# One gated mixer, regrouped: each output tile behind one block of products, and the next weights' sums in one piece at a block's end

## The chip, the cores and the metric

The kernel runs on one core of one Trainium2 chip. The metric is the device time of one execution in microseconds (us). The kernel before took 2506.31 us in the median of three runs (2504.49 to 2506.65). The engines are named as the profile names them: PE multiplies matrices (PEld loads its weights), DVE and POOL do elementwise work, ACT applies functions and copies, and SP issues the transfers from memory.

## The reference, cut to what matters

The program is one inference step of a decoder trunk of two layers, for 1024 prompt tokens and 64 sample tokens, with 1024 channels. After the token mixer, each layer applies a gated channel mixer:

```python
def swiglu(h, w_in, w_out):
    g, u = jnp.split(h @ w_in, 2, axis=-1)
    return (jax.nn.silu(g) * u) @ w_out

# in each layer, with FFN_DIM = 2816
h = h + mix
h = h + swiglu(rms_norm(h, norm_ffn_g[layer]), w_ffn_in[layer], w_ffn_out[layer])
```

The change concerns this mixer in layer 1 alone, and there only the first group of tokens.

## The kernel before, in words

**Groups and tiles.** The tokens are worked on in two groups: group A, 512 tokens, and group B, 576 tokens. Activations lie with channels on the 128 partitions. The 2816 hidden channels are 22 tiles f of 128; two tiles form a pair q, so there are 11 pairs, 0 to 10. `run_ffn` (L460) loops over the pairs. For each pair it computes both hidden tiles, and then adds the pair before it into the result: the tile `hid` of pair q-1 is multiplied by two output weight tiles of 512 channels (o = 0 and 1). Each of these takes four accumulators of 128 channels, six matmuls of 512 columns each, 24 matmuls for one output tile. DVE adds each accumulator to the running sum `hb` (`added`, L297).

**A block of products.** Group A of layer 1 computes g and u of one hidden tile by a seven-product scheme in place of eight (`strassen`, L518): each product is 12 matmuls of 256 columns (L525), 84 for one block. The seven products land in four accumulator tiles X (two), Y (two), Z (two) and W (one), in this order. DVE combines them by seven additions (`add`, L529), ACT copies one of them out of PSUM first (L541), and ACT applies SiLU at the end (L554). The product of the gate and u (L504) is made on POOL later, by a list of postponed pieces that `flush` empties; a further `flush` copies it into `hid` as a high part (ACT, L240) and a low part (DVE, L241). One flush stands behind X in each block, one in the output part.

**Accumulators.** There are three accumulator buffers in PSUM, taken in turn. W takes X's buffer; the fourth accumulator of an output tile takes the buffer of its first.

**Weights.** SP loads each weight tile (512 KB) into one of four `stage` buffers (L166). The kernel works in float32 split into two parts, so each weight is split before use into a high part (a copy on ACT) and a low part (a subtraction on POOL of the high part from the weight), in one of three `hl` buffers. `w_split` does this. For output weights this is one ACT copy (L184) and two POOL subtractions (L186). For a block of products the weights come as four steps r0 to r3, one for X, Y, Z and W, since the scheme multiplies sums of weights: r0 first needs three sums on DVE (L200, L201, L202) of the two staged tiles g and u, then two copies on ACT (L196) and two subtractions on POOL (L197). r1 and r2 need two of each, r3 one more DVE sum (L214, `sum_c`) and one of each. L186, L197 and L504 are all POOL instructions of 128x512. In all POOL does ten of them for one block and one output tile.

**Order.** Every engine works through its instructions in the order in which the program writes them. `w_next` takes the weights of a step and at the same time writes the splitting of the step two further on. So the r0 of a pair's second block is written at Z of its first block, ahead of the DVE additions there. In the output part a flag, `thin`, makes the three sums of the next r0 single pieces, one behind each of the first three accumulators of the output tile o = 0. The list `seq` fixes the order of the weights, and with it the order of the loads: four loads of input weights for a pair, and then two of output weights.

Layer 0 and group B go through the same functions, but the change leaves their order alone.

Of the kernel before, what the change touches and what calls it, by code (L numbers as in the profile page):

```python
# [57 lines left out]
def trunk_kernel(ctx, tc, x_prompt, x_sample, cache_k, cache_v, state_conformer, state_shortconv, state_pool,  # L58
# [59 lines left out]

    def add_ffn(l, plain, both=True):
        for g in range(NF // 2):  # L120
            for f in (2 * g, 2 * g + 1):
                if f < plain:
                    add_in(w_ffn_in[l], f * 128)
                    add_in(w_ffn_in[l], FFN + f * 128)
                else:
                    a = in_load(w_ffn_in[l], f * 128), in_load(w_ffn_in[l], FFN + f * 128)
                    seq.extend(a + (r,) for r in range(4))
            if g and (g < NF // 2 - 1 or not both):
                for o in range(2):
                    add_out(w_ffn_out[l], g - 1, o)  # L130
        for o in range(2):
            if both:
                add_out(w_ffn_out[l], NF // 2 - 2, o)
            add_out(w_ffn_out[l], NF // 2 - 1, o)
# [87 lines left out]
    def w_next(live=0):  # L222
        j = wj[0]
        wj[0] += 1
        w_split(j + 3 - live)
        w_load(need(j + 6 - live))
        return hls.pop(j)
# [67 lines left out]
    def added(g, dst, acc):  # L295
        for a, d in parts(g, acc, dst):
            dve.tensor_tensor(d, a, d, op=OP.add)  # L297
# [162 lines left out]
    def run_ffn(g, accs, ps, hidp, x, last, sig=False, slot=lambda: None, forms=None, plain=NF,  # L460
# [54 lines left out]

        def strassen(f):  # L518
            w2 = n // 2

            def prod(acc, h, i, b):
                for k in range(4):
                    xk = forms[b](k)
                    for s, (wi, xi) in enumerate(((0, 0), (0, 1), (1, 0))):
                        pe.matmul(acc[:, :w2], h[:, wi, i, k], xk[:, xi], start=k == 0 and s == 0,  # L525
                                  stop=k == 3 and s == 2)

            def add(out, acc, x):
                dve.tensor_tensor(out, acc[:, :w2], x, op=OP.add)  # L529

            a, b = slice(0, w2), slice(w2, n)
            X, h = accs(), w_next()
            prod(X[:, 0], h, 0, "t2")
            prod(X[:, 1], h, 1, "t3")
            flush()
            slot()
            Y, h = accs(), w_next()
            prod(Y[:, 0], h, 0, "t1")
            prod(Y[:, 1], h, 1, "b11")
            G_, U, P = tmp(), tmp(), tmp()  # L540
            act.activation(G_[:, a], Y[:, 1, :w2], AF.Copy)  # L541
            Z, h = accs(), w_next()
            prod(Z[:, 0], h, 0, "t4")
            add(U[:, a], X[:, 0], G_[:, a])
            add(U[:, b], X[:, 1], U[:, a])
            add(P[:, b], Y[:, 0], U[:, b])
            add(G_[:, b], Y[:, 0], U[:, a])
            prod(Z[:, 1], h, 1, "b21")
            W, h = accs(), w_next()
            prod(W[:, 0], h, 0, "b22")  # L550
            add(P[:, a], Z[:, 0], U[:, b])
            add(G_[:, a], Z[:, 1], G_[:, a])
            add(G_[:, b], W[:, 0], G_[:, b])
            act.activation(G_[:, :n], G_[:, :n], AF.Silu)  # L554
            gated(f, P, G_)
            slot()

        for q in range(G + 1):
            if q < G:
                for f in (2 * q, 2 * q + 1):  # L560
                    if f >= plain:
                        if f == plain:
                            forms.get("switch", forms.get("ready"))()
                        strassen(f)
                        continue
                    if f == 0 and not done:
                        run_in(g, accs, x, [ev_g, lambda a: ev_u(0, a)], norm_hooks(g, ps, at=(4, 7)), skew=3)
                        slot()
                        continue
                    one(f, 0)  # L570
                    one(f, 1)
            if q == G - 1:
                free()
                if both:
                    return last([hid.pop(q - 1), hid.pop(q)])
            if q == G:
                flush()
                flush()
                last(hid.pop(q - 1))
            elif q:  # L580
                hh = hid.pop(q - 1)
                for o in range(2):
                    thin[0] = True
                    h = w_next()
                    thin[0] = False
                    for i in range(4):
                        a = accs()
                        out_block(g, a, h, i, hh)
                        added(g, hb[:, o * 4 + i, g.cs], a)
                        if parts_:  # L590
                            parts_.pop(0)()
                        if o == 0 and i == 1:
                            flush()
                        slot()
# [45 lines left out]
    def accs():  # L640
        return accbox["p"].tile([128, len(accbox["g"].blocks), 512], F, name="acc")
# [1392 lines left out]
```

## Time and profile before

| | us |
|---|---|
| median of three runs | 2506.31 |
| the profiled execution, time | 2507.39 |
| the profiled execution, span | 2505.6 |
| PE busy in it | 2420.9 |
| pairs 1 to 9 of layer 1's group A (1742.05 to 2043.17 of the span) | 301.12 |

The pairs 1 to 9 are those that the change reorders. A pair begins where PE begins the 36 matmuls of X and of Y's first product and ends at the same place of the next pair. A row of a timeline gives start, duration, engine, line, operation, what it writes and reads, and a count where several alike are merged; in square brackets stand the idle time before it and what ended it. In a group of instructions the columns behind the count are the total busy time, the mean of one in ns, and the idle time ahead of them with its releasers. Since DVE's and POOL's instructions can hold each other up, the duration that a row gives can include a wait inside the instruction.

### The profile page before, as it was taken

To read this page: it belongs to the slowest core of one execution; us is meant where nothing else is said; L and a number is where in the kernel's file an instruction comes from. 1 tells how busy PE (TensorE), PEld (TensorE's weight loads), DVE (VectorE), ACT (ScalarE), POOL (GpSimd) and SP (SyncE) were. 2 spreads that over 40 slices of the span, in tenths; PEclk is the share of its full clock that TensorE was granted. 3 is DMA by queue.
4 is the path that set the end of the run, shared out by engine and by line. 5 is a ranking of instruction groups with operands and counts; after the bars stand their busy time and mean duration, and the time that the engine had idled before them with its cause. 6 is when DMAs were issued, how large, how long until landed. Compare 5 with 4: busy or idle time off the path is not lost.

```text
span 2505.6 us, 41453 instructions
## 1 busy us (share of the span) xinstructions
PE 2420.9 (97%) x15877; PEld 2190.0 (87%) x15877; DVE 1653.7 (66%) x2288; ACT 1106.5 (44%) x1877; POOL 1625.1 (65%) x1264
## 2 busy tenths in 40 slices
PE   8999999999999999999999999998999999999998
PEld 6788877788777679999999999888888888999998
DVE  3696878977777553766566534458777668666655
ACT  5536876754444343343333422234333444443333
POOL 6764334655654576787787523267888886887775
PEclk9999999999999999999999999999999999999999
DMA  7332231234565534223232311242233323233322
GB/s 226 117 108 73 77 111 48 72 103 144 175 180 172 160 93 148 71 74 98 89 100 86 111 49 43 71 139 68 85 101 102 98 90 92 85 98 114 93 85 81
DMA packets 355485, 258.31 MB, mean 103 GB/s; under 512 B 22913, under 2 KB 303617, under 8 KB 355272
## 3 DMA queue, kind: packets, MB, share of 16 engines
q1 hardware_dynamic: 355256, 255.66, 34.5%
q8 instruction: 126, 2.06, 0.3%
q14 instruction: 71, 0.58, 0.1%
q10 hardware_dynamic: 32, 0.01, 0.0%
HBM read 237.41 MB, written 18.69 MB: 102 GB/s over the span
## 4 chain that ended last, share of the span: by engine, by line
PE 73%; DVE 16%; POOL 4%; issue 3%; ACT 3%; DMA 1%; SPq 0%; DVEq 0%; ACTq 0%; POOLq 0%
PE acc L235 44%; PE acc L525 20%; DVE sum L200 1%; POOL hl L197 1%; DVE hb L297 1%; DVE q L1008 1%; POOL hl L186 1%; PE o L1030 1%; DVE hid L241 1%; PE m L1020 1%; PE m L1132 1%; PE z L991 1%; DVE sum L201 1%; PE z L1155 1%; DVE cacc L831 1%
## 5 line engine op out<-in xcount | busy, mean ns | idle before, releaser
L186 POOL TENSOR_TENSOR hl<-stage,hl 128x512 fp32r<-128x512 f32 x464 | 637.8, 1399 | 389.3 <-ACT hl L184 280.9
L235 PE MATMUL acc<-x,hl 128*128 128x512 f32 (+1 forms) x3648 | 773.5, 350 | 11.2 <-DVE tmp L293 3.0
L235 PEld LDWEIGHTS acc<-x,hl 128*128 128x128 f32 x3648 | 587.9, 190 | 75.1 <-issue 5.8
L235 PE MATMUL acc<-hid,hl 128*128 128x288 f32 (+1 forms) x3096 | 548.2, 333 | 10.8 <-DVE tmp L293 4.6
L235 PEld LDWEIGHTS acc<-hid,hl 128*128 128x128 f32 x3096 | 471.0, 189 | 62.9 <-DVE hb L297 7.2
L297 DVE TENSOR_TENSOR hb<-acc,hb 128x512 f32<-128x512 f32 (+1 forms) x360 | 256.3, 718 | 173.1 <-PE acc L235 171.7
L525 PE MATMUL acc<-x,hl 128*128 128x288 f32 (+1 forms) x2676 | 361.9, 290 | 3.0 <-POOL hl L197 2.4
L525 PEld LDWEIGHTS acc<-x,hl 128*128 128x128 f32 x2676 | 348.6, 188 | 5.3 <-POOL hl L197 3.3
L197 POOL TENSOR_TENSOR hl<-sum,hl 128x512 fp32r<-128x512 f32 x180 | 237.7, 1349 | 169.3 <-ACT hl L196 169.3
L184 ACT ACTIVATE hl<-stage 128x1024 fp32r<-128x1024 f32 x232 | 243.8, 1054 | 228.6 <-PE acc L235 145.8
L529 DVE TENSOR_TENSOR tmp<-acc,tmp 128x288 f32<-128x288 f32 (+1 forms) x420 | 173.6, 441 | 230.6 <-ACT tmp L541 136.2
L197 POOL TENSOR_TENSOR hl<-stage,hl 128x512 fp32r<-128x512 f32 x180 | 268.4, 1513 | 14.4 <-ACT hl L196 14.4
L525 PE MATMUL acc<-b,hl 128*128 128x256 f32 (+1 forms) x1548 | 215.7, 290 | 14.1 <-DVE tmp L529 11.2
L525 PEld LDWEIGHTS acc<-b,hl 128*128 128x128 f32 x1548 | 201.3, 188 | 19.8 <-ACT hl L196 12.6
L235 PE MATMUL acc<-x1t,hl 128*128 128x288 f32 x1152 | 216.3, 296 | 1.5 <-POOL hl L186 1.5
L235 PEld LDWEIGHTS acc<-x1t,hl 128*128 128x128 f32 x1152 | 195.9, 188 | 19.5 <-POOL hl L186 1.8
L196 ACT ACTIVATE hl<-sum 128x512 fp32r<-128x512 f32 x180 | 103.0, 623 | 238.1 <-DVE sum L202 217.6
L293 DVE TENSOR_TENSOR tmp<-acc,rr 128x512 f32<-128x512 f32 (+1 forms) x108 | 75.2, 710 | 136.3 <-PE acc L235 122.4
L196 ACT ACTIVATE hl<-stage 128x512 fp32r<-128x512 f32 x180 | 105.5, 618 | 69.4 <-PE acc L235 59.3
L504 POOL TENSOR_TENSOR tmp<-tmp 128x576 f32<-128x576 f32 (+1 forms) x85 | 126.2, 1485 | 9.2 <-ACT tmp L481 8.2
L252 POOL TENSOR_TENSOR ss<-ss,tmp 128x512 f32<-128x512 f32 (+1 forms) x69 | 108.1, 1566 | 25.5 <-ACT tmp L251 15.2
L235 PE MATMUL acc<-x1a,hl 128*128 128x512 f32 x480 | 121.7, 407 | 2.5 <-POOL hl L186 1.3
(298 smaller groups left out, 3166.5 us busy)
## 6 DMA issues: line engine op xcount, KB each, us to landing
stage<-in_w_ffn_in_dram SPq DMA_DIRECT2D x176, 512.0 KB
stage<-in_w_ffn_out_dram SPq DMA_DIRECT2D x88, 512.0 KB
stage<-in_w_in_even_dram SPq DMA_DIRECT2D x40, 512.0 KB
kst<-in_cache_k_dram SPq DMA_DIRECT2D x64, 256.0 KB
vst<-in_cache_v_dram SPq DMA_DIRECT2D x56, 256.0 KB
stage<-in_w_out_even_dram SPq DMA_DIRECT2D x16, 512.0 KB
stage<-in_w_in_odd_dram SPq DMA_DIRECT2D x16, 512.0 KB
stage<-in_w_out_odd_dram SPq DMA_DIRECT2D x16, 512.0 KB
```

Source lines behind the costliest of these rows:

```text
L184: act.activation(hl[:, 0], st, AF.Copy)
L186: pool.tensor_tensor(hl[:, 1, c], st[:, c], f32(hl[:, 0, c]), op=OP.subtract)
L196: act.activation(hl[:, 0, c], x, AF.Copy)
L197: pool.tensor_tensor(hl[:, 1, c], x, f32(hl[:, 0, c]), op=OP.subtract)
L200: todo = [lambda: dve.tensor_tensor(sb, su[:, lo], su[:, hi], op=OP.add), lambda: dve.tensor_tensor(sa[:, hi], sg[:, lo], su[:, lo], op=OP ...
L235: pe.matmul(acc[:, b, :c1 - c0], w, xs[:, xi, c0 - o:c1 - o], start=first and s == 0, stop=last and s == 2)
L252: pool.tensor_tensor(ss[:, g.cs], ss[:, g.cs], t[:, :g.n], op=OP.add)
L293: dve.tensor_tensor(d, a, r, op=OP.mult)
L297: dve.tensor_tensor(d, a, d, op=OP.add)
L504: (dve if both and f == NF - 1 else pool).tensor_tensor(t[:, :n], t[:, :n], u[:, :n], op=OP.mult)
L525: pe.matmul(acc[:, :w2], h[:, wi, i, k], xk[:, xi], start=k == 0 and s == 0, stop=k == 3 and s == 2)
L529: dve.tensor_tensor(out, acc[:, :w2], x, op=OP.add)
```

## The change

In layer 1's group A, for the pairs 1 to 9:

- Each output tile of pair q-1 stands behind one block of products: the first behind the first block of pair q, the second behind the second (`out_tile`), where both stood behind the second block. `seq`, and so the order of loads, follows: two input tiles, one output tile, and so on.
- The three sums for the next block's r0 are held back at W (`thin`) and written together at the end of the block, behind its seven additions and the SiLU, ahead of the output tile. The copies and the subtractions of r0 follow them there.
- The splitting of r1 is written behind the second accumulator of the output tile, and a flush behind the third.
- In the first block of pair 1 one more flush stands ahead of W, so that pair 0 is in `hid` when the output tile behind that block reads it.

```diff
     def add_ffn(l, plain, both=True):
         for g in range(NF // 2):
+            outs = g and (g < NF // 2 - 1 or not both)
             for f in (2 * g, 2 * g + 1):
 ...
                     seq.extend(a + (r,) for r in range(4))
-            if g and (g < NF // 2 - 1 or not both):
+                if outs and l and both:
+                    add_out(w_ffn_out[l], g - 1, f % 2)
+            if outs and not (l and both):
                 for o in range(2):
                     add_out(w_ffn_out[l], g - 1, o)
 ...
-        def strassen(f):
+        def out_tile(hh, o):
+            h = w_next(1)
+            for i in range(4):
+                a = accs()
+                out_block(g, a, h, i, hh)
+                added(g, hb[:, o * 4 + i, g.cs], a)
+                if i == 1:
+                    w_split(wj[0] + 2)
+                if i == 2:
+                    flush()
+                slot()
+
+        def strassen(f, outs=False):
 ...
             prod(Z[:, 1], h, 1, "b21")
+            if outs and f == 2:
+                flush()
+            thin[0] = outs
             W, h = accs(), w_next()
+            thin[0] = False
 ...
             gated(f, P, G_)
+            if outs:
+                while parts_:
+                    parts_.pop(0)()
             slot()
 
         for q in range(G + 1):
+            alt = done and both and 0 < q < G - 1
 ...
-                        strassen(f)
+                        strassen(f, alt)
+                        if alt:
+                            out_tile(hid[q - 1], f % 2)
                         continue
 ...
+            elif alt:
+                hid.pop(q - 1)
             elif q:
                 hh = hid.pop(q - 1)
```

On DVE, one pair of the kernel before, from the sums that stand ahead of the first block's additions (the names are the tiles: `stage` is a loaded weight tile, `sum` a sum of two, `tmp` the products' combinations, `acc` an accumulator, `hb` the running result):

```order
L200 TENSOR_TENSOR sum_19125<-stage 128x512
L201 TENSOR_TENSOR sum_19124<-stage 128x512
L202 TENSOR_TENSOR sum_19124<-sum_19125,stage 128x512
L529 TENSOR_TENSOR tmp<-acc,tmp 128x256 x7
L214 TENSOR_TENSOR sum_c<-stage,sum_19124 128x512
L529 TENSOR_TENSOR tmp<-acc,tmp 128x256 x7
L297 TENSOR_TENSOR hb<-acc,hb 128x512
L200 TENSOR_TENSOR sum_19313<-stage 128x512
L297 TENSOR_TENSOR hb<-acc,hb 128x512
L201 TENSOR_TENSOR sum_19312<-stage 128x512
L241 TENSOR_TENSOR hid<-tmp,hid 128x512
L297 TENSOR_TENSOR hb<-acc,hb 128x512
```

The third sum (L202) and five more additions to `hb` follow. In the changed kernel, one block and its output tile read so on DVE (L544 is what L529 was, L203 to L205 the three sums, L300 the addition to `hb`, L217 `sum_c`, L244 the low part of `hid`):

```order
L544 TENSOR_TENSOR tmp<-acc,tmp 128x256 x7
L203 TENSOR_TENSOR sum_19160<-stage 128x512
L204 TENSOR_TENSOR sum_19159<-stage 128x512
L205 TENSOR_TENSOR sum_19159<-sum_19160,stage 128x512
L300 TENSOR_TENSOR hb<-acc,hb 128x512 x4
L217 TENSOR_TENSOR sum_c<-stage,sum_19159 128x512
L244 TENSOR_TENSOR hid<-tmp,hid 128x512
```

The sums moved from ahead of seven additions (first block) and from between the additions to `hb` (output part) to one place behind the additions, and every block is like the next.

On POOL, one pair of the kernel before (L197 with `sum` and `stage` are the low parts of r0, r1 and r2, with `sum_c` that of r3, L186 those of the two output weight tiles, L504 the gate times u):

```order
L197 TENSOR_TENSOR hl<-sum_20676,hl 128x512 x2
L197 TENSOR_TENSOR hl<-sum_20677,hl 128x512
L197 TENSOR_TENSOR hl<-stage,hl 128x512 x3
L197 TENSOR_TENSOR hl<-sum_c,hl 128x512
L197 TENSOR_TENSOR hl<-sum_20829,hl 128x512 x2
L197 TENSOR_TENSOR hl<-sum_20830,hl 128x512
L197 TENSOR_TENSOR hl<-stage,hl 128x512 x3
L504 TENSOR_TENSOR tmp<-tmp 128x512
L197 TENSOR_TENSOR hl<-sum_c,hl 128x512
L186 TENSOR_TENSOR hl<-stage,hl 128x512 x4
L504 TENSOR_TENSOR tmp<-tmp 128x512
```

And one block with its output tile in the changed kernel (L200, L189 and L507 are what L197, L186 and L504 were):

```order
L189 TENSOR_TENSOR hl<-stage,hl 128x512 x2
L200 TENSOR_TENSOR hl<-sum_20353,hl 128x512 x2
L200 TENSOR_TENSOR hl<-sum_20354,hl 128x512
L200 TENSOR_TENSOR hl<-stage,hl 128x512
L507 TENSOR_TENSOR tmp<-tmp 128x512
L200 TENSOR_TENSOR hl<-stage,hl 128x512 x2
L200 TENSOR_TENSOR hl<-sum_c,hl 128x512
```

POOL has 20 instructions for a pair in both. Four output-weight subtractions in a row became two and two, each pair of them just ahead of the next r0.

## The prediction

> **What bounds the kernel now.** First the page's head, for the whole program:
>
> ```profile
> span 2505.6 us, 41453 instructions
> PE 2420.9 (97%) x15877; PEld 2190.0 (87%) x15877; DVE 1653.7 (66%) x2288; ACT 1106.5 (44%) x1877; POOL 1625.1 (65%) x1264
> ```
>
> PE is busy nearly throughout, so a change of order can only win back PE's gaps, and only where it acts. So the second view is busy time in windows, one for each of the nine pairs that are reordered, from one pair's first matmul to the next's (columns: length; busy time and count of PE, PEld, DVE, ACT, POOL; clock; transfers):
>
> ```profile
> 1742.05:1777.42 35.37, 33.08 (x222) 29.68 (x221) 25.27 (x35) 15.73 (x27) 32.22 (x23) 1.00 0.31 90
> ...
> 1846.63:1879.08 32.45, 31.82 (x217) 28.81 (x216) 22.28 (x32) 12.94 (x22) 27.93 (x21) 1.00 0.33 98
> 1879.08:1912.36 33.28, 32.24 (x218) 28.78 (x216) 23.65 (x32) 12.94 (x22) 26.95 (x21) 1.00 0.33 96
> ...
> sum 301.12, PE 289.58 PEld 260.31 DVE 216.84 ACT 119.25 POOL 253.83; mean PE 32.18 PEld 28.92 DVE 24.09 ACT 13.25 POOL 28.20
> ```
>
> The nine take 301.12 us, 18 blocks with an output tile of 16.73 each. The clock is 1.00. The three pairs up to 1846.63 take 104.58 and the six behind them 196.54, 32.76 each. What would PE need alone?
>
> ```profile
> 1867.58 11.66 PE L235 MATMUL acc<-hid,hl 128*128 128x512 f32 x48
> 1889.90 4.39 PE L525 MATMUL acc<-x,hl 128*128 128x256 f32 x36
> 1894.12 1.57 PE L525 MATMUL acc<-b,hl 128*128 128x256 f32 x12
> ```
>
> 48 matmuls of 512 columns run from 1867.58 to the pair's end at 1879.08, 11.50 or 0.2396 each; 36 of 256 columns run from 1889.90 to 1894.12, 4.22 or 0.1172 each. One block is 84 x 0.1172 = 9.84, one output tile 24 x 0.2396 = 5.75, both 15.59; 18 of them 280.6, with a few small matmuls of the next group's norm some 282. So 19 us stand between the nine pairs and PE alone: the most that the change can win. The waits of PE's matmuls in these windows name DVE first:
>
> ```profile
> PE acc L525 <- DVE tmp L529: 7.8, 10, 1.7
> PE acc L235 <- DVE hb L297: 2.2, 4, 0.8
> PE acc L525 <- POOL hl L197: 0.9, 2, 0.5
> ```
>
> These 10.9 us are the visible part (weight loads that start late and slower matmuls behind them make the rest). They name W, which waits for DVE to release X's accumulator. But a wait at W is only where PE notices; something has to hold the whole loop at 32.5 to 33.3. The groups of POOL's instructions in these windows show it:
>
> ```profile
> L197 POOL TENSOR_TENSOR hl<-stage,hl 128x512 fp32r<-128x512 f32 x54 | 79.8, 1504 | 0.0
> L197 POOL TENSOR_TENSOR hl<-sum,hl 128x512 fp32r<-128x512 f32 x56 | 77.0, 1405 | 47.3 <-ACT hl L196 47.3
> L186 POOL TENSOR_TENSOR hl<-stage,hl 128x512 fp32r<-128x512 f32 x36 | 45.5, 1298 | 0.0
> L504 POOL TENSOR_TENSOR tmp<-tmp 128x512 f32<-128x512 f32 x19 | 28.3, 1487 | 0.0
> L197 POOL TENSOR_TENSOR hl<-sum_c,hl 128x512 fp32r<-128x512 f32 x18 | 27.3, 1516 | 0.0
> ```
>
> These are 183 instructions, 180 of them those of nine pairs (20 a pair, the rest at the edges), and in the last row of the windows POOL is busy 253.83 of 301.12. All its idle time, 47.3, stands ahead of one group, r0's subtractions:
>
> ```profile
> POOL hl L197 <- ACT hl L196: 47.3, 17, 4.4
> ```
>
> Everywhere else POOL runs back to back. So these pairs are bound by POOL's chain: its busy time plus the pause ahead of each r0. PE's stalls follow from it.
>
> **What an instruction and a pause of POOL cost.** POOL's timeline over a pair's end:
>
> ```profile
> 1879.90 4.71 POOL L197 TENSOR_TENSOR hl<-stage,hl 128x512 fp32r<-128x512 f32 x3
> 1884.56 1.74 POOL L197 TENSOR_TENSOR hl<-sum_c,hl 128x512 fp32r<-128x512 f32 x1
> ...
> 1898.74 5.05 POOL L186 TENSOR_TENSOR hl<-stage,hl 128x512 fp32r<-128x512 f32 x4
> 1903.76 1.29 POOL L504 TENSOR_TENSOR tmp<-tmp 128x512 f32<-128x512 f32 x1
> 1909.43 3.81 POOL L197 TENSOR_TENSOR hl<-sum,hl 128x512 fp32r<-128x512 f32 x3 [4.38 <-ACT hl L196]
> ```
>
> and DVE's at the same time:
>
> ```profile
> 1879.89 1.86 DVE L214 TENSOR_TENSOR sum_c<-stage,sum 128x512 f32<-128x512 f32 x1
> 1881.67 1.78 DVE L241 TENSOR_TENSOR hid<-tmp,hid 128x512 fp32r<-128x512 f32 x1
> 1883.37 1.78 DVE L200 TENSOR_TENSOR sum<-stage 128x512 f32<-128x512 f32 x1
> ...
> 1890.10 0.42 DVE L529 TENSOR_TENSOR tmp<-acc,tmp 128x256 f32<-128x256 f32 x1 [0.33 <-PE acc L525]
> ...
> 1902.48 3.12 DVE L200 TENSOR_TENSOR sum<-stage 128x512 f32<-128x512 f32 x1
> 1905.52 0.68 DVE L297 TENSOR_TENSOR hb<-acc,hb 128x512 f32<-128x512 f32 x1
> 1906.12 0.67 DVE L201 TENSOR_TENSOR sum<-stage 128x512 f32<-128x512 f32 x1
> 1906.72 0.68 DVE L241 TENSOR_TENSOR hid<-tmp,hid 128x512 fp32r<-128x512 f32 x1
> ...
> 1907.92 0.68 DVE L202 TENSOR_TENSOR sum<-sum,stage 128x512 f32<-128x512 f32 x1
> ```
>
> Four L186 take 5.05 together: 1.26 each when undisturbed. An L197 of the same shape takes 1.74 at 1884.56, while DVE reads two tiles from SBUF (L200 from 1883.37, 1.78 long against 0.68 for the same shape at 1907.92). They keep each other out: DVE waits for POOL's instruction to end, and POOL then loses 1.74 - 1.29 = 0.45 to DVE's. Three L197 with two such insertions (L214, L241) take 4.71: 3 x 1.26 + 2 x 0.46. I take 0.45. The check: 180 x 1.26 = 227 of 253.83 busy us leaves 27 for 59 insertions of 0.45, out of 18 x 5 + 8 such DVE instructions; the others fall into the pauses.
>
> The rule of the Trainium skill, "SBUF — State Buffer", section "Who interferes with whom", is that a DVE instruction with two SBUF inputs and a GpSimd instruction that reads SBUF take the pair of ports in turn, for the whole instruction. The trace agrees that they exclude each other, but not on the price: 0.45, not the 0.68 of the DVE instruction.
>
> The pause: at 1905.05 POOL ends L504 and stands idle to 1909.43, 4.38 us, because DVE works L201, L241, L202 and two hb additions in between (from 1906.12 to 1908.60) ahead of r0. From L202's end to POOL's start, through ACT's copy, is 0.83.
>
> **The change, part by part.**
>
> *POOL's instructions:* the same 180, 227 us (180 x 1.263).
>
> *Insertions:* the three sums of a block now stand where POOL waits for them, and cost inside the pause. Left to hit POOL at work are sum_c and hid's low part, two a block: 36 x 0.45 = 16.2. The eight pieces of the next group's norm stay too:
>
> ```profile
> L1705 DVE SCALAR_TENSOR_TENSOR xs<-hb,par,rr 128x576 f32<-128x576 f32 x8 | 9.9, 1236 | 0.0
> ```
>
> With 576 columns in place of 512 I put 0.51 on each, 4.1 together. From 26.5 to 20.3: minus 6.2.
>
> *The pause ahead of r0:* by program order POOL ends the output weights' second subtraction, then waits for three sums and ACT. A DVE sum that stands ready ends 0.54 behind POOL's instruction (L200 ends at 1885.15, the three L197 at 1884.61); then 0.60 for each further one (from 1906.12 to 1906.72), and 0.8 to POOL's start (the 0.83, rounded): 0.54 + 0.60 + 0.60 + 0.8 = 2.54, 18 times 45.7, in place of 47.3: minus 1.6. Below: if sums get in between the last two subtractions, 3 x 0.45 + 0.83 = 2.18, 6.5 less in all. Above: the 4.38 of the row, if other DVE work got in between, 33 more; order gives the three sums nothing in between, so I take 2.54.
>
> This needs the sums to be ready to start when POOL ends those subtractions. One block from X's start, with PE held by POOL's low parts: W ends at 9.85 and DVE's last addition some 0.6 later (in the rows, W ends where the next product starts, at 1889.90, and the addition that waited for it at 1890.52), at 10.5. POOL, counted from r2's second low part, which the third matmul of Z's second product needs at 62 x 0.1172 = 7.3, does r3 (to 8.5) and the two output subtractions (9.8 and 11.05). So DVE is ready at 10.5 and POOL free at 11.05; 0.55 to spare. The loop of POOL alone is 10 x 1.263 + 2 x 0.45 + 2.54 = 16.1, above PE's 15.6: POOL stays the bound, and PE will still wait about 0.5 in each, for POOL now.
>
> *W's wait:* the additions no longer stand behind three sums on DVE, so W finds X's buffer free. That wait goes, 7.8 us of PE's, but is no gain of its own: what is late next is the low part of r2 or of an output tile.
>
> *The output additions behind the sums:* the fourth accumulator of an output tile waits for the first one's hb addition, now queued on DVE behind the three sums. They end at 11.05 + 1.74 = 12.8 and it, with the 0.68 of L297, at 13.5; PE comes to the fourth at 9.85 + 3 x 1.44 = 14.2. Hidden by 0.7; if the sums were 1 later, 0.3 an output tile.
>
> *Loads:* SP's order becomes two input tiles and one output tile. The later input tile takes the buffer that r2's first low part frees (at 7.3 - 1.26 - 0.45 = 5.6), and behind its wait in SP's queue stand one output tile and the next input tile. It is needed at 11.05, 5.4 later. A load alone: SP issues one at
>
> ```profile
> 1871.27 0.37 SPq L166 DMA_DIRECT2D stage<-in_w_ffn_in_dram  x1
> ```
>
> and the transfer engines right behind it (the last two columns are their busy share and GB/s):
>
> ```profile
> 1872.00:1872.50 0.50, 0.50 (x4) 0.41 (x3) 0.50 (x2) 0.00 (x0) 0.50 (x1) 1.00 0.09 27
> ...
> 1874.00:1874.50 0.50, 0.50 (x3) 0.38 (x3) 0.50 (x2) 0.00 (x0) 0.00 (x0) 1.00 0.87 260
> 1874.50:1875.00 0.50, 0.50 (x3) 0.24 (x2) 0.50 (x2) 0.00 (x0) 0.00 (x0) 1.00 0.02 5
> ```
>
> so the data has ended 3.3 us after the issue. The load is hidden by 2 us, and if that cover goes, each us beyond 5.4 costs 18.
>
> *The extra flush and the earlier splitting of r1* move one ACT copy and one DVE piece of the same size, once, or the same instructions within the tile: nothing, since ACT is busy 119 of 301 and the hid piece is counted above.
>
> **Sum:** 227.3 + 20.3 + 45.7 = 293.3 in place of 301.1: minus 7.8. On the profiled span of 2505.6 that is 2497.8 (2507.39 less 7.8 is 2499.6 for the profiled execution's time); on the median of 2506.31 it is **2498.5 us**.
>
> **The rivals.**
>
> *PE alone becomes the bound.* The sums slip in between POOL's last subtractions and the pauses shrink to 2.18 or below; then 15.6 a block, 282 for the pairs, 19 less: 2487; with 2.18 alone 2492. For it: 0.55 us is little to spare. Against it: the sums wait for W, and W for PE, so an earlier POOL doesn't bring them forward. Chance 0.10.
>
> *The time moves and is not won.* The additions end 0.6 later than counted, behind a starved hid piece (L200 waited over 2 us at 1902.48), and the sums with them: a pause of 3.0 in place of 2.54 and the loop at 16.6 to 16.7, as now: 2506. For it: POOL's chain with ten instructions is untouched, and PE's wait at W was never the bound. Chance 0.20.
>
> *The insertion costs DVE's whole 0.68.* 227.3 + 44 x 0.68 + 45.7 = 302.9, 1.8 more than now: 2508. That is what the Trainium skill's page "SBUF — State Buffer" would make of it. Against it: the 4.71 for three. Chance 0.05.
>
> *The load comes too late: slower.* The output tile's load is issued 1.3 to 1.7 behind the input tile's, and if the transfer engines share themselves between the two, the first ends with the second. Then the sums wait at the head of DVE's queue with the hb additions behind them. From 6.1 us for the load it is slower than before (5.4, and 0.65 for the gain of a block); at 6.5, 1.1 x 18 = 20 on top of the 293.3: 2518. For it: before, these loads were issued long ahead of their sums in the first block. Against it: 3.3 alone. Chance 0.10.
>
> **How the numbers follow.** The forecast has 0.55, with a range of its own from 2494 to 2503 (0.2 more or less in each block's pause is 3.6 us). The range from 2489 to 2509 takes in no change and the smaller pause, and leaves out most of the late load and the PE bound. About 0.2% (5 us) is what a measurement of this kernel tells from no change. Faster by more: 0.46 of the forecast and the 0.10 of the PE bound, 0.56. Within it: 0.09, 0.20, 0.04, 0.33. Slower: 0.11.
>
> **What would show it.** In the changed profile: the nine pairs take 293 us and are alike behind the third, 32.2 each. POOL's idle time stands still ahead of r0 alone, 2.5 each time and 18 times, none of 4.4. The waits of L525's matmuls for DVE are gone and those for POOL have grown to some 5 to 9 us. The three sums stand at 0.55 to 0.7 each, with no 1.77 among them. Wrong would be: PE waiting for DVE at the fourth accumulator, a DVE sum that starts late behind a load, or pauses as long as before with the pairs at 33.

## The result: 5.8 us faster, a ratio of 0.9977

The changed kernel takes 2501.11 us in the median of 21 runs (2499.06 to 2506.25), the kernel before, in runs beside it, 2506.94 in the median of 21 (2503.79 to 2511.53). The ratio is 0.9977, with a 95% interval from 0.9971 to 0.9983: 5.8 us faster where 7.8 were forecast, 2501.1 against a forecast of 2498.5. Its profiled execution took 2503.01 with a span of 2501.2.

The head of the page after:

```profile
span 2501.2 us, 41461 instructions
PE 2423.2 (97%) x15877; PEld 2194.5 (88%) x15877; DVE 1625.4 (65%) x2288; ACT 1105.2 (44%) x1877; POOL 1618.3 (65%) x1264
```

The windows of the nine reordered pairs after, from the same start to pair 10's first matmul (columns as in the prediction):

```profile
1742.05:1777.01 34.96, 34.96 (x227) 32.30 (x227) 21.04 (x35) 15.83 (x27) 28.07 (x21) 0.93 0.31 91
...
1842.97:1875.07 32.10, 32.07 (x218) 29.14 (x216) 19.71 (x32) 12.98 (x22) 26.94 (x21) 1.00 0.33 99
...
2003.50:2035.61 32.11, 32.05 (x217) 28.98 (x216) 19.81 (x32) 12.81 (x22) 26.95 (x21) 1.00 0.35 99
sum 293.56, PE 291.66 PEld 264.38 DVE 184.78 ACT 118.40 POOL 245.42; mean PE 32.41 PEld 29.38 DVE 20.53 ACT 13.16 POOL 27.27
```

From the fourth pair on every pair takes 32.1, where before they ran from 32.45 to 33.28. But the first row is long, 34.96 at a clock of 0.93. PE's timeline around its start shows that it holds something that isn't its own:

```profile
1740.55 2.90 PE L540 MATMUL acc<-b,hl 128*128 128x256 f32 x12 [2.73 <-DVE tmp L544]
1743.25 5.96 PE L540 MATMUL acc<-x,hl 128*128 128x256 f32 x36
```

The first row is W of pair 0, behind a wait that the kernel before has as well, at the same place and as long. There these 12 matmuls took 1.66; here they took 2.90, at half the clock, so that pair 1's X begins at 1743.25 and not at 1742.05. The nine pairs themselves, from PE's first matmul of X in pair 1 to that in pair 10 ("X to X" below), take 2035.61 - 1743.25 = 292.36.

Pair 10, which the change leaves in the old order, is the other surprise. Its windows from X's first matmul to the first output matmul, before:

```profile
2043.17:2064.20 21.03, 20.37 (x169) 19.97 (x168) 13.96 (x20) 9.59 (x16) 19.08 (x15) 1.00 0.31 100
```

and after:

```profile
2035.61:2059.99 24.38, 22.08 (x169) 21.51 (x168) 13.03 (x20) 9.53 (x16) 22.37 (x18) 0.93 0.29 87
```

So the two profiled spans differ as follows (us):

| stretch | before | after | difference |
|---|---|---|---|
| W of pair 0, slower at a low clock | 0 | 1.20 | +1.20 |
| pairs 1 to 9, X to X | 301.12 | 292.36 | -8.76 |
| pair 10, X to its output | 21.03 | 24.38 | +3.35 |
| all the rest | | | -0.19 |
| span | 2505.6 | 2501.2 | -4.4 |

(The profiled execution after lay 1.9 above its median and the one before 0.45 above, which makes the -5.8 of the medians out of -4.4.)

**Inside a pair.** The groups of POOL's and DVE's instructions after, those that answer to the prediction's:

```profile
L200 POOL TENSOR_TENSOR hl<-stage,hl 128x512 fp32r<-128x512 f32 x54 | 84.9, 1586 | 0.0
L200 POOL TENSOR_TENSOR hl<-sum,hl 128x512 fp32r<-128x512 f32 x55 | 71.9, 1338 | 47.4 <-ACT hl L199 47.4
L189 POOL TENSOR_TENSOR hl<-stage,hl 128x512 fp32r<-128x512 f32 x36 | 46.3, 1307 | 0.8 <-ACT hl L187 0.8
...
L507 POOL TENSOR_TENSOR tmp<-tmp 128x512 f32<-128x512 f32 x18 | 23.7, 1316 | 0.0
L200 POOL TENSOR_TENSOR hl<-sum_c,hl 128x512 fp32r<-128x512 f32 x18 | 23.3, 1293 | 0.0
...
L203 DVE TENSOR_TENSOR sum<-stage 128x512 f32<-128x512 f32 x18 | 17.0, 944 | 0.0
```

POOL's idle time still stands ahead of r0 almost alone: 47.4 over 18 blocks, 2.6 each, where it was 47.3. What has shrunk is its busy time: X to X it is 244.22, from 253.83 (the 245.42 of the windows above begins 1.20 earlier). PE's matmuls no longer wait for DVE in these pairs:

```profile
PE acc L540 <- POOL hl L200: 1.3, 3, 0.5
```

What PE waits for is POOL, and mostly at its weight loads:

```profile
PEld acc L540 <- POOL hl L200: 7.8, 30, 0.7
```

The timeline of one block's end, with POOL's pause (X began at 1939.29; engines mixed, in order of time):

```profile
1940.99 1.75 POOL L200 TENSOR_TENSOR hl<-stage,hl 128x512 fp32r<-128x512 f32 x1
...
1943.94 3.01 POOL L200 TENSOR_TENSOR hl<-stage,hl 128x512 fp32r<-128x512 f32 x2
...
1944.68 1.10 DVE L244 TENSOR_TENSOR hid<-tmp,hid 128x512 fp32r<-128x512 f32 x1 [3.10 <-ACT hid L243]
...
1945.26 0.37 SPq L169 DMA_DIRECT2D stage<-in_w_ffn_in_dram  x1
...
1948.16 2.55 POOL L189 TENSOR_TENSOR hl<-stage,hl 128x512 fp32r<-128x512 f32 x2
...
1949.73 5.77 PE L238 MATMUL acc<-hid,hl 128*128 128x512 f32 x24
1949.93 0.42 DVE L544 TENSOR_TENSOR tmp<-acc,tmp 128x256 f32<-128x256 f32 x1 [0.68 <-PE acc L540]
1950.27 0.98 DVE L203 TENSOR_TENSOR sum<-stage 128x512 f32<-128x512 f32 x1
...
1951.17 0.68 DVE L204 TENSOR_TENSOR sum<-stage 128x512 f32<-128x512 f32 x1
1951.78 0.68 DVE L205 TENSOR_TENSOR sum<-sum,stage 128x512 f32<-128x512 f32 x1
1952.38 1.27 DVE L300 TENSOR_TENSOR hb<-acc,hb 128x512 f32<-128x512 f32 x2
...
1953.28 3.81 POOL L200 TENSOR_TENSOR hl<-sum,hl 128x512 fp32r<-128x512 f32 x3 [2.58 <-ACT hl L199]
```

POOL ends its last subtraction at 1948.16 + 2.55 = 1950.71 and stands still until 1953.28, 2.58 by the row. DVE's last addition (the row at 1949.93) ends at 1950.35, so the first sum is ready ahead of POOL's end, waits for it, and ends at 1951.25; the other two follow 0.6 apart.

### The profile page after: what moved, and what is told of

The parts are those of the page before. It is cut to its first block, busy times and chain, and to the rows that moved or that the text cites. A ratio compares the mean times of both kernels' runs of the same rounds, so it can differ in the third digit from the quotient of the medians.

```text
span 2501.2 us, 41461 instructions
## 1 busy us (share of the span) xinstructions
PE 2423.2 (97%) x15877; PEld 2194.5 (88%) x15877; DVE 1625.4 (65%) x2288; ACT 1105.2 (44%) x1877; POOL 1618.3 (65%) x1264
## 4 chain that ended last, share of the span: by engine, by line
PE 72%; DVE 12%; POOL 4%; ACT 3%; issue 3%; SPq 0%; DMA 0%; DVEq 0%; ACTq 0%; POOLq 0%
PE acc L238 41%; PE acc L540 23%; POOL hl L200 2%; DVE q L1035 1%; PE o L1057 1%; DVE hb L300 1%; PE m L1159 1%; PE m L1047 1%; PE z L1182 1%; PE z L1018 1%; POOL hl L189 1%; DVE be L1037 1%; DVE sum L203 1%; DVE hid L244 1%; DVE sum L204 1%
## 5 line engine op out<-in xcount | busy, mean ns | idle before, releaser
L189 POOL TENSOR_TENSOR hl<-stage,hl 128x512 fp32r<-128x512 f32 x464 | 637.8, 1398 | 393.6 <-ACT hl L187 279.9
L540 PE MATMUL acc<-x,hl 128*128 128x288 f32 (+1 forms) x2676 | 368.0, 291 | 5.8 <-POOL hl L200 3.7
L300 DVE TENSOR_TENSOR hb<-acc,hb 128x512 f32<-128x512 f32 (+1 forms) x360 | 255.6, 718 | 171.1 <-PE acc L238 169.8
L200 POOL TENSOR_TENSOR hl<-sum,hl 128x512 fp32r<-128x512 f32 x180 | 233.4, 1325 | 170.3 <-ACT hl L199 168.3
L544 DVE TENSOR_TENSOR tmp<-acc,tmp 128x288 f32<-128x288 f32 (+1 forms) x420 | 174.7, 442 | 210.6 <-ACT tmp L556 106.3
L200 POOL TENSOR_TENSOR hl<-stage,hl 128x512 fp32r<-128x512 f32 x180 | 273.9, 1540 | 14.1 <-ACT hl L199 14.1
L507 POOL TENSOR_TENSOR tmp<-tmp 128x576 f32<-128x576 f32 (+1 forms) x85 | 123.6, 1454 | 9.1 <-ACT tmp L484 8.1
L244 DVE TENSOR_TENSOR hid<-tmp,hid 128x576 fp32r<-128x576 f32 (+1 forms) x66 | 78.5, 1192 | 72.0 <-ACT hid L243 72.0
```

The lines of the kernel that those rows point to most:

```text
L189: pool.tensor_tensor(hl[:, 1, c], st[:, c], f32(hl[:, 0, c]), op=OP.subtract)
L200: pool.tensor_tensor(hl[:, 1, c], x, f32(hl[:, 0, c]), op=OP.subtract)
L244: (on or dve).tensor_tensor(dst[:, 1], src, f32(dst[:, 0]), op=OP.subtract)
L507: (dve if both and f == NF - 1 else pool).tensor_tensor(t[:, :n], t[:, :n], u[:, :n], op=OP.mult)
```

## The experiments

The theory on trial: these pairs are bound by POOL's chain, its instructions plus the pause ahead of r0, and the gain is what the new place of the sums takes out of that chain. The main rival: the gain is W's wait, which is gone. Later runs look for what pair 10 gave back, and whether what is learned makes a faster kernel. The line numbers in the rows move by a few with each edit.

**1. Only W's wait taken away, in the kernel before.** The three sums of the second block stand behind the first four additions of the first block, where they stood ahead of them. They are held back when Z's weights are taken and written when W's are:

```diff
             act.activation(G_[:, a], Y[:, 1, :w2], AF.Copy)
+            thin[0] = bool(done and both and f % 2 == 0 and 1 < f < 2 * (G - 1))
             Z, h = accs(), w_next()
+            thin[0] = False
```

> The kernel before, with one thing changed: in the first block of pairs 1 to 9 the three sums stand behind the first four additions instead of ahead of all seven, so that the additions that release W's accumulator are no longer behind them. If PE's wait at W (7.8 us in the nine pairs) is what the change won, this wins 4 to 8 us: about 2500. If POOL's chain is the bound, the sums now come later to r0 (from about 1886.9 in place of 1883.4, done about 1888.7 in place of 1887.45) and the pause ahead of r0 grows by some 1.2 us in each pair: about 11 us slower, 2518, with the wait at W gone all the same.

Measured: 2520.17, ratio 1.0049 [1.0035, 1.0062], 13 us slower. PE's waits in the pairs:

```profile
PE acc L525 <- POOL hl L197: 8.4, 12, 0.9
PE acc L525 <- ACT hl L196: 5.5, 9, 1.6
...
PE acc L525 <- DVE tmp L529: 0.5, 1, 0.5
```

PE's waits for DVE at these matmuls have gone from 7.8 to 0.5, and the kernel is slower. POOL's pause has grown, since the sums, and with them r0, come later:

```profile
POOL hl L197 <- ACT hl L196: 68.4, 18, 4.4
```

from 47.3 to 68.4. The nine pairs have grown from 301.1 to 314.9 (1741.06 to 2055.91). So the wait at W went down by 7.3 and the time up by 13.7, which is what POOL's chain makes of it: its pauses grew by 21.1, and its busy time fell by 7.4 (246.48 from 253.83), so POOL is again busy or paused ahead of r0 all the time. The rival falls in the form on record: taking W's wait away does not by itself win 4 to 8 us. Since the edit also makes r0 later, it can't show alone that POOL sets the pace; the next two runs test that.

**2 and 3. One more POOL instruction a block, in the kernel before and in the changed one.** One low part of r1 is worked out twice in each block of the nine pairs, with the same result:

```diff
 ...
-                    cut(src=(sb, sg[:, lo]) if r == 1 else ...)
+                    if r == 1 and a in again:
+                        cut(src=(sb, sg[:, lo]))
+                        pool.tensor_tensor(hl[:, 1, hi], sg[:, lo], f32(hl[:, 0, hi]), op=OP.subtract)
+                    else:
+                        cut(src=(sb, sg[:, lo]) if r == 1 else ...)
```

> The kernel before with one subtraction of r1 done twice on POOL in each of the 18 blocks (the same values written again): 11 POOL instructions a block in place of 10. If POOL's chain is the bound, all of 18 x 1.26 = 23 us comes on top: 2529 (at least 15 us, if some of the long pauses take it up). If PE with its wait at W is the bound and POOL's pauses of 47 us are slack, 0 to 5 us.

> The changed kernel with the same subtraction of r1 done twice on POOL in each of the 18 blocks. If POOL's chain is still the bound after the change (16.1 a block against PE's 15.6), 18 x 1.26 = 23 us on top: about 2523. If PE had become the bound, the 0.5 of slack a block would be used first: 14 us or less, 2515.

Measured: before with it 2529.18, ratio 1.0082 [1.0067, 1.0098], 21.8 slower than before. The change with it 2524.38, ratio 1.0071 [1.0055, 1.0086], so 23.3 above the change (22.9 when each is taken against the kernel before in its own runs, since the change was not run beside it). X to X the nine pairs take 322.57 (1744.32 to 2066.89) and 315.37 (1740.25 to 2055.62), 21.5 and 23.0 more than without the instruction. Eighteen instructions at 1.26 are 22.7: both kernels pay about the whole price, so in both POOL's chain is the bound. Two blocks' beginnings in the steady stretch of the changed kernel with it:

```profile
1864.30 4.39 PE L546 MATMUL acc<-x,hl 128*128 128x256 f32 x36
...
1881.71 4.39 PE L546 MATMUL acc<-x,hl 128*128 128x256 f32 x36
```

A block takes 1881.71 - 1864.30 = 17.41 where the change alone took 16.05 (half of 32.1).

**4. The changed kernel without holding the sums back.** They stand at W's weights again, ahead of the additions; everything else is as in the change:

```diff
-            thin[0] = outs
+            thin[0] = False
             W, h = accs(), w_next()
```

> The changed kernel with one part undone: the sums are not held to the block's end but stand at W, ahead of the last three additions (order of output tiles and loads as changed). If the place of the sums matters as I think, they alternate there with POOL's subtractions and the last three additions come at 13 to 14 us of a block, so that the second accumulator of the output tile waits 1.5 to 2 us: 10 to 25 us slower than the kernel before, 2516 to 2530. If only the alternation of blocks and output tiles counts, the time is that of the change, 2501.

Measured: 2510.07, ratio 1.0010 [1.0000, 1.0019], 9 us above the change (8.6 when each is taken against the kernel before in its own runs). So without this one part the whole gain is lost, but the size was expected far too large. PE's row in one block shows the mechanism:

```profile
1939.80 1.56 PE L238 MATMUL acc<-hid,hl 128*128 128x512 f32 x6
1942.04 4.48 PE L238 MATMUL acc<-hid,hl 128*128 128x512 f32 x18 [0.68 <-DVE tmp L544]
```

The second accumulator of each output tile waits for the additions that stand behind the sums:

```profile
PE acc L238 <- DVE tmp L544: 14.3, 17, 1.7
```

0.84 a tile. Of the three sums only the second was held up by POOL for as long as in the kernel before:

```profile
1938.94 1.77 DVE L204 TENSOR_TENSOR sum<-stage 128x512 f32<-128x512 f32 x1
```

A steady block takes 16.5 here, 0.47 more than in the change, and X to X the nine pairs take 302.24 (1743.33 to 2045.57), 9.9 more. Pair 10, which follows, takes 21.07 (2045.57 to 2066.64), 3.3 less than in the change; the next experiment comes back to that.

**5 and 10. What pair 10 gives back.** In the kernel before, in pair 10's first block, DVE and PE did this (rows of the timeline; L241 is the low part of `hid`, L200 the first of the three sums):

```profile
2043.17 4.43 PE L525 MATMUL acc<-x,hl 128*128 128x256 f32 x36
...
2045.76 1.78 DVE L241 TENSOR_TENSOR hid<-tmp,hid 128x512 fp32r<-128x512 f32 x1
...
2047.46 1.78 DVE L200 TENSOR_TENSOR sum<-stage 128x512 f32<-128x512 f32 x1
...
2052.48 1.66 PE L525 MATMUL acc<-b,hl 128*128 128x256 f32 x12 [0.61 <-DVE tmp L529]
```

and after (L244 and L203 are the same two):

```profile
2035.61 4.39 PE L540 MATMUL acc<-x,hl 128*128 128x256 f32 x36
...
2041.01 1.10 DVE L244 TENSOR_TENSOR hid<-tmp,hid 128x512 fp32r<-128x512 f32 x1 [3.09 <-ACT hid L243]
...
2042.03 1.78 DVE L203 TENSOR_TENSOR sum<-stage 128x512 f32<-128x512 f32 x1
...
2047.05 2.90 PE L540 MATMUL acc<-b,hl 128*128 128x256 f32 x12 [2.27 <-DVE tmp L544]
```

The low part of `hid` starts 2.59 behind X before (2045.76 less 2043.17) and 5.40 behind it after (2041.01 less 2035.61). In the nine pairs it stands there too, at 1944.68 with X at 1939.29, and costs nothing, since the sums come only at the block's end. In pair 10, whose first block keeps the old order, the three sums and the additions stand behind it on DVE, and W waits 2.27 where it waited 0.61. Behind that wait the clock drops:

```profile
2046.00:2047.00 1.00, 0.00 (x0) 0.00 (x0) 0.86 (x3) 0.80 (x2) 0.04 (x1) 1.00 0.75 246
2047.00:2048.00 1.00, 0.95 (x4) 0.98 (x5) 1.00 (x3) 1.00 (x3) 1.00 (x1) 0.52 0.21 82
...
2050.00:2051.00 1.00, 1.00 (x8) 1.00 (x8) 1.00 (x2) 0.56 (x2) 1.00 (x2) 0.77 0.00 0
```

(the whole stretch from 2047 to 2051 lies below 1.00), so W's 12 matmuls take 2.90 in place of 1.66. From start to start, the longer wait makes 1.66 of the 3.35, W's slowness 1.19 (2.69 from W to the next block against 1.50), and the two products ahead of them 0.47 (their rows are 1.82 and 1.88 against 1.57 and 1.60); the second block is about as long as before.

The experiment moves the last flush of the nine pairs up, from behind the third accumulator to behind the first, ahead of r1's splitting, and only for the last output tile of pair 9:

```diff
-        def out_tile(hh, o):
+        def out_tile(hh, o, at=2):
 ...
+                if i == at == 0:
+                    flush()
                 if i == 1:
                     w_split(wj[0] + 2)
-                if i == 2:
+                if i == at == 2:
                     flush()
 ...
-                            out_tile(hid[q - 1], f % 2)
+                            out_tile(hid[q - 1], f % 2, 0 if f == 2 * G - 3 else 2)
```

> The changed kernel with one flush moved: in the last reordered output tile (behind the second block of pair 9) it stands behind the first accumulator instead of the third, so that POOL makes that block's gate times u ahead of r1's subtractions and not behind them. In the changed kernel the first block of pair 10, which kept the old order, waits 2.3 us at W, since the low part of hid comes 5.4 us behind X's start (2.6 before) and the three sums and the additions stand behind it on DVE. If that is the cause of the 3.3 us that pair 10 gives back, the wait at W falls to 0.6 and 1.5 to 3 us come back: 2498 to 2499.5, and PE's clock stays at 1.00 there. If the loads' new order is the cause (the sums wait for a late load), nothing changes: 2501.

Measured: 2499.25, ratio 0.9958 [0.9945, 0.9971]. Its pair 10:

```profile
2036.35:2058.40 22.05, 21.40 (x170) 20.22 (x168) 14.81 (x20) 9.72 (x16) 22.05 (x17) 1.00 0.31 93
```

It takes 22.05 in place of 24.38, with the clock at 1.00 throughout. DVE's low part of `hid` starts at 2038.82, 2.47 behind X (2036.35), and W no longer waits. It is still 1.02 longer than before the change, as PE now waits for POOL's low parts there (0.29 at one place, and rows of 1.86 and 1.85 against 1.57). The difference in medians from the change was still to be had on one chip:

> The changed kernel with the last reordered output tile's flush behind its first accumulator, now beside the changed kernel on one chip. By the trace it won 2.3 us in pair 10 (from 24.4 to 22.05, 1.2 of it by a clock that stayed at 1.00, which need not fall in each execution): 1 to 2.5 us less than the changed kernel. If pair 10's loss is an accident of one profile: no difference.

> The changed kernel as it is, on the same chip and beside the same runs of the kernel before as the next one: 0.9977 of the kernel before, 5 to 6 us less. It is the base for the kernel with the one flush moved.

Measured side by side: the change again 2502.09 (8 runs), ratio 0.9976 [0.9965, 0.9986]; the early flush 2499.43 (5 runs), ratio 0.9963 [0.9950, 0.9977]. That is 2.7 less, but the intervals overlap, so the times alone don't settle it. The profiles do for pair 10: 24.41 in the change again (2035.63 to 2060.04), with the same wait of 2.27, and 22.04 with the early flush (2035.79 to 2057.83). The nine pairs of the change again took 292.47, X to X.

**6. The product of gate and u on DVE in the nine pairs, in the changed kernel.** If POOL is the bound, taking away one of its ten instructions should gain until PE's 15.59 a block is reached:

```diff
-                (dve if both and f == NF - 1 else pool).tensor_tensor(t[:, :n], ...)
+                (dve if both and (f == NF - 1 or done and 1 < f < NF - 2) else pool).tensor_tensor(t[:, :n], ...)
```

> The changed kernel with one instruction of each of the 18 blocks moved: the gate times u (128x512) on DVE instead of POOL, 9 POOL instructions a block in place of 10, and one more insertion of 0.45 by DVE. If POOL's chain is the bound, a block's loop falls from 16.1 to 15.3, below PE's 15.6, so PE takes over: the nine pairs at 281 to 283, 10 to 12 us less than the change, 2489 to 2491. If what bounds it is something else (DVE's order, the load behind r2's first subtraction), the time stays at 2501 or gets longer.

Measured: 2489.54, ratio 0.9924 [0.9909, 0.9938], 11.6 below the change (13.6 when each is taken against the kernel before in its own runs). Two starts of X in a row:

```profile
1930.82 4.43 PE L540 MATMUL acc<-x,hl 128*128 128x256 f32 x36
...
1946.39 4.43 PE L540 MATMUL acc<-x,hl 128*128 128x256 f32 x36
```

15.58 apart: PE's own floor of 15.59, as the prediction worked it out from before's rows. POOL's pause grew (50.9, X to X, from 47.4 in the change), without cost, since POOL is no longer the bound.

**7. Both together**, the early flush and the product on DVE:

> The two edits above together. If they are independent, their gains add: 12 to 15 us less than the change, 2486 to 2489. If the late hid piece at the end of pair 9 only came from POOL being behind, the first edit adds nothing to the second: 2489 to 2491.

Measured: 2487.9, ratio 0.9917 [0.9904, 0.9931], the fastest of all, 19 us below the kernel before in the medians (21.0 in the same runs). Whether the early flush adds to the sixth experiment the times leave open: 1.6 apart, with intervals that overlap. The profiles say that it adds next to nothing in pair 10: 21.70 (2023.40 to 2045.10) against 21.89 (2024.30 to 2046.19) in the sixth. There, with the product on DVE alone, the low part of `hid` already starts 2.36 behind X, and W waits 1.49; here W waits 1.29. That fits the second expectation, that the late piece of `hid` came from POOL being behind.

**8. The same product on DVE, in the kernel before**, to see what the change itself is worth when POOL has one instruction less:

> The kernel before (order not changed) with the same 18 products on DVE instead of POOL. If POOL's chain bounds the old order as well, each block loses 1.26 and gains 0.45: up to 14 us less, about 2493, if the pauses ahead of r0 stay as long as they are. If the pauses are set by DVE's pieces between the output additions, the additional DVE work lengthens them and less than 5 us are left: 2502 to 2507.

Measured: 2499.33, ratio 0.9960 [0.9946, 0.9974], 9.6 faster than before, between the two expectations. POOL's pause tells why:

```profile
POOL hl L197 <- ACT hl L196: 61.6, 17, 5.7
```

It grew by 14.3, from 47.3, and 22.7 (what 18 instructions took out of POOL) less 14.3 is 8.4: just what the nine pairs lost, 292.73 (1740.87 to 2033.60) in place of 301.12. The pauses that grew are those behind the output weights' subtractions: 4.98 each in the last six pairs, where they were 3.17 to 4.38. Before, POOL's product (L504) stood just ahead of that pause; now it stands inside it on DVE (0.68 long, between L201 and L241, ahead of r0's last sum). So most of what was taken out of POOL's busy time there came back as pause; how much of it is DVE's added work isn't shown. In the changed order the pause grows by 3.5 alone, and the nine pairs of the sixth experiment take 283.21 (1741.09 to 2024.30), 17.9 less than before: about the sum of the two parts, 8.76 for the change and 8.4 for the product.

## Why the prediction was right, and where its sum missed

**The bound was right.** The second and third experiments show it directly: 18 more POOL instructions cost 21.8 and 23.3, about their 22.7, before and after the change. The rival of PE alone as the bound fell with that; it came true only when an instruction was taken off POOL (15.58 a block, in the sixth).

**The nine pairs came out near the sum, but in part by luck.** Forecast 293.3, measured 292.4 (292.5 in the second profile). Two terms missed in opposite directions. The 253.83 of POOL's busy time before is that of 183 instructions, and the prediction set only 180 against it: with 183 x 1.263 some 22.7 were insertions, not 26.5. After, 244.2 less the 227.3 of 180 instructions leaves 16.9, where 20.3 was forecast. The pauses came to 48.2 in all (47.4 and the 0.8 ahead of L189), where 45.7 was forecast, so the 1.6 that they were to win did not come. That is 3.4 too much in one term and 2.5 too little in the other. What the change did win on POOL is insertions, 5.8 by this count where 6.2 was forecast; the other 3.8 that its busy time fell are three instructions that no longer lie between the two starts of X, which the step that failed comes back to. The size of an insertion was near: from the fourth pair on 26.94 a pair less 20 x 1.263 leaves 0.42 for each of four, and the rows of 1.75 and 3.01 show 0.49. An insertion at DVE's whole 0.68 was a rival; it fell. The pause of 2.54 was measured at 2.58 in the steady blocks. The loop 16.1, measured 16.05. DVE's last addition ends 11.06 behind X and POOL 11.42, where the working said 10.5 and 11.05: the cover is 0.36 and not 0.55, but it held. The rival by which the time only moves had the additions 0.6 late, and they were 0.56 late; but POOL's subtraction was 0.37 later too. That rival fell by about a third of a microsecond a block.

**W's wait is gone and was no gain of its own**, as the prediction said: in the first experiment it went as well, and the time grew with POOL's chain.

**What was costed at nothing in the pairs was nothing.** The fourth accumulator waits in none of the steady blocks: the first addition to `hb` ends at about 1953.0, 13.7 behind X, and PE comes to the fourth at 1949.73 + 18 x 0.2396 = 1954.04, 14.75 behind. The load for the next sums is issued at 1945.26, 5.97 behind X (5.6 was worked out), and the sum at 1950.27 doesn't wait for it. So neither the late load nor a wait at the fourth accumulator came about.

**Two of the signs were a little off.** PE's waits for POOL came to 7.8 as foretold (5 to 9), but at the weight loads; the matmuls themselves show 1.3. And the first sum takes 0.94 in the mean, not 0.55 to 0.7, since it starts ahead of POOL's end and waits inside the instruction, which is the 0.55 that the pause was worked out with; there is none of 1.77.

**The step that failed** is the one on the extra flush and the moved splitting: "the same instructions within the tile: nothing". Within the nine pairs that holds. But the sum ended with pair 9, and the flush of its last output tile sets when the low part of `hid` reaches DVE in pair 10: 5.40 behind X, not 2.59. In the nine pairs the moved sums are the cover for that. Pair 10's first block is in the old order and has no such cover: +3.35. The fifth and tenth runs show it: with that flush alone moved up, pair 10 takes 22.05 and 22.04, and the wait and the drop of the clock are gone; 1.0 of the 3.35 stays.

The flush is not alone in it. In the fourth experiment it stands at the same place, but the sums are not held, and there the low part of `hid` starts 2.79 behind X in pair 10 (2048.36 less 2045.57) and W waits 0.62. With the sums held, POOL starts r0 later beside PE: 3.55 behind the start of the output tile (1953.28 less 1949.73) where it is 2.34 without (1942.14 less 1939.80). At X of pair 10 its three subtractions from sums had 0.87 us to run before (they end at 2044.04) and 1.76 after (2037.37), and the product of gate and u (1.28 at 2039.03), done by then before, was still ahead. So about 2.2 us of POOL's work that the sum counted in the nine pairs was passed on to pair 10, and that part of the 8.76 is work that left the stretch and was not saved; how much of the 3.35 it makes isn't shown. (The rest of the 3.8 lies at the stretch's start: POOL had 2.6 us of its subtractions from sums left at X before, and 0.9 at the later X of this profile.)

The ledger then reads -8.76 + 3.35 = -5.4, beside -5.8 of the medians; the 1.2 of W in pair 0 comes in some executions and not in others.

**The sizes that I misjudged in the experiments.** Without holding the sums back 2516 to 2530 were expected and 2510 came: the mechanism (an accumulator that waits for additions behind the sums) is there, at 0.84 a tile. And the product on DVE in the kernel before gained 9.6, between the two expectations on record: neither had counted by how much the pause would grow.

## What to carry to other kernels

A wait at the busiest engine names the place where it notices, not what sets the pace: add one instruction to the engine you suspect, and see whether the whole loop pays. Work on a loop's chain as instructions plus pauses, and put work that an engine waits for into one piece inside the pause, not across that engine's busy time. And where a loop is reordered and its neighbour is not, work out what the last turn hands over, and when: the neighbour may lack the cover that made the new place free.

## What the runs showed of the hardware that was not expected

A pause of PE of 1.9 to 2.7 us was followed by half the clock, but not every time. W of pair 0 waits 2.73 in both kernels. The windows around its end, before:

```profile
1740.00:1742.00 2.00, 1.45 (x12) 1.48 (x13) 1.82 (x5) 1.98 (x5) 1.59 (x2) 1.00 0.00 0
```

and after:

```profile
1740.00:1742.00 2.00, 1.45 (x7) 1.48 (x8) 1.82 (x5) 1.98 (x5) 1.59 (x2) 0.50 0.00 0
...
1746.00:1748.00 2.00, 2.00 (x17) 2.00 (x16) 1.47 (x1) 0.27 (x2) 2.00 (x2) 0.83 0.00 0
```

The same 12 matmuls took 1.66 before and 2.90 after, and the clock was back only within the window from 1746 to 1748. In the second profile of the change the same wait (2.74) left them at 1.66. In pair 10 a wait of 2.27 was followed by the low clock in both profiles of the change, and without the wait (the fifth experiment) it stayed at 1.00. A shorter pause further on did the same in the kernel before, where the 18 matmuls behind it took 6.02, with the clock at 0.50 from 2088 to 2090:

```profile
2085.84 6.02 PE L235 MATMUL acc<-hid,hl 128*128 128x512 f32 x18 [1.85 <-DVE hb L297]
```

In the changed kernel they took 4.47 behind a pause of 1.86. Behind the six waits of 1.67 at W in the second experiment, W took 1.66 or 1.67 each time.

In pair 0 the slow clock reached into pair 1, whose X took 5.96 where it took 4.39 in the second profile. Yet the nine pairs were no longer for it (292.36 and 292.47): POOL sets their pace.

The Trainium skill, "TensorE: Matmul & The Clock Gate", section "HAM oscillation — how this bites in real kernels", warns of PE-idle gaps above some 3.4 us; these runs show that shorter ones can be followed by it. That the window which watches PE runs freely, as the same page of the Trainium skill says under "What's actually happening", would fit a drop in one execution and none in the next, but no run here shows the window. For a forecast it means that a new wait of about 2 us on PE can have a price of 1.2 us or more beside its own length, some of the time.
